# Experts' gate applied between their products, weight splits made at first use and tied behind the next input's chain, router's second rows in another buffer

## Chip, cores and metric

The kernel runs on one core of a Trainium2 chip. The metric is the time of one execution in microseconds (us) on the device. A core has a matrix engine (PE), three engines for elementwise work (DVE, ACT, POOL), and queues that issue transfers (SP's carries nearly all weights). Each engine works through its own instructions in the order in which the program lists them; semaphores hold an instruction until what it reads is there.

## The reference

Two networks one behind the other, on 256 rows of 1024 fp32 values:

```python
def first_block(x, mem, ...):
    h = rms_norm(x, attn_norm)
    ...                                   # attention, rwkv7, memory attention on h @ w_in
    x = x + mixed @ w_out
    xn = rms_norm(x, ffn_norm)
    return x + hierarchical_moe(xn, ...)

def hierarchical_moe(xt, ...):            # gate: [T, 16], two experts of one group per row
    for e in range(N_EXPERTS):
        hdn = silu(xt @ w_gate[e]) * (xt @ w_up[e])
        y = y + gate[:, e:e + 1] * (hdn @ w_down[e])
    return y

def swiglu(x, w1, w3, w2):
    return (silu(x @ w1) * (x @ w3)) @ w2
```

The second network adds six branches to the rows, each on its own rms_norm of them: a SwiGLU feed-forward of 2816 (ffn0), a mixer with 16 heads (hyb: dilated attention and top-k attention), ffn1, ffn2, a sliding-window attention (swa), ffn3. A last norm ends it.

## The kernel before

**Data.** The running rows are two tiles `h[0]`, `h[1]` of 128 x 1024 (`h_81`, `h_82` in the order's rows). All products keep fp32's accuracy by three matmuls (`mm3`, L105 to L107): each operand is a rounded high part and the rest, and the product is high x high, high x low, low x high. For the weights, `load` fetches a `raw` tile of 128 x 4096 through SP into a ring of three, and `split` cuts it into pieces of 1024 columns: ACT casts `wh` (L99), DVE subtracts to get `wl` (L100). A small ring of buffers holds the split pieces.

**Input of a branch.** `prep(...).fill(t)` makes a branch's input from `h[t]`: for each half `a` of its columns, PE transposes four blocks into a PSUM bank (L133), DVE multiplies by the norm's gain into `xf` (L139), ACT casts the high part `xh` (L140), DVE subtracts to get `xl` (L141). There are two such banks (`tr`), so the transposes of `h[1]` wait until `xf` of `h[0]` has been read out of them. Then ACT squares `h[t]` for the norm's divisor (L119). The divisor itself is applied later, where the product leaves PSUM.

**End of a branch.** `project_back` multiplies by the branch's last matrix, in an order of row blocks; the last `tail` of them (6 for all branches of the second network) are kept back, done for `h[0]` first and then for `h[1]`. Behind each, DVE adds the product to `h[t]` (L399, or L401 with a scale) and `after(t)` calls the next branch's `fill(t)`. It is a generator, and its first part (all but the tail) is started from `staggered`, which interleaves a mixer's head groups.

**Experts.** `moe` runs the 16 experts as eight pairs, each pair's 128 gathered rows as one tile. `first(p)` makes SiLU (ACT, L1348) times the up product (DVE, L1349) in `es`, transposes it into `eT`; `second(p, kept)` multiplies by the down matrix into two banks `po` (L1366), multiplies by the row's gate into `yf` (DVE, L1373), splits that in `yr` (cast on ACT L1374, subtraction on DVE L1375), and PE adds it back to the rows' places through the 0/1 matrix `PT` (L1380). After the eighth pair `add` adds the four sums to `h` (L1391), past a branch (L1401) that reads whether an expert overflowed its 64 slots.

**Order.** The program is written in Python order, but a scheduler with a model of the engines decides where an instruction stands in its engine's list. That list is fixed when the kernel is built.

## Time and profile before

| | |
|---|---|
| time, median of 3 runs | 1412.01 us (1409.84 to 1412.82) |
| time of the profiled execution | 1412.13 us |
| its span | 1410.4 us |
| PE busy | 1355.6 us (96%) |
| DVE busy | 743.6 us (53%) |
| ACT busy | 610.3 us (43%) |
| PE's idle time (span less busy) | 54.8 us |

The profile is of one execution. Its span is what the views divide; 1.7 us of the time lie around it. The branches lie in the span so: first network to 429 us (the experts from about 216), ffn0 to 630, hyb to 757, ffn1 to 945, ffn2 to 1131, swa to 1216, ffn3 to 1403.

### The profile page before, as it was taken

The page shows a single profiled execution, that of the slowest core. Times are in us where ns is not written, and L with a number is a line of the kernel's source. Part 1 is how long each engine was busy: PE and PEld are TensorE (multiplying, and loading weights), DVE is VectorE, ACT ScalarE, POOL GpSimd, SP SyncE. Part 2 cuts the span into 40 slices and gives each one's busy share as a digit, 9 for nine tenths or more (in the row PEclk, how much of TensorE's full clock was granted, in tenths as well). Part 3 has the DMA queues.
Part 4 walks back from the last instruction along what each step waited for, and adds up shares of the span by engine and source line. Part 5 has one row for each costly group of instructions (what it writes and reads, how often), then busy time and mean ns, then how long its engine had stood idle before and what let it go on. Part 6 is the DMA issues. An engine that isn't in the chain of part 4 may idle for free.

```text
span 1410.4 us, 18949 instructions
## 1 busy us (share of the span) xinstructions
PE 1355.6 (96%) x7650; PEld 1040.8 (74%) x7650; DVE 743.6 (53%) x1250; ACT 610.3 (43%) x961; POOL 73.9 (5%) x123
## 2 busy tenths in 40 slices
PE   7999889999998999999899999999999989999997
PEld 7787664343335888888787888888888878788886
DVE  6868641111126555456965555455545487555542
ACT  5545421011114444446565444445444376554442
POOL 1133100000000000000110000000000000000001
PEclk9999889999998999999999999999999999999999
DMA  8262579999964555446433555455554543355520
GB/s 318 91 236 92 211 285 412 412 415 425 425 277 180 185 180 199 157 157 254 150 120 127 202 181 207 150 186 198 206 183 152 209 164 135 140 210 183 199 90 30
DMA packets 35372, 293.82 MB, mean 208 GB/s; under 512 B 3729, under 2 KB 8113, under 8 KB 16081
## 3 DMA queue, kind: packets, MB, share of 16 engines
q1 hardware_dynamic: 29952, 286.58, 53.6%
q10 hardware_dynamic: 5328, 5.98, 1.3%
q8 instruction: 62, 1.02, 0.3%
q14 instruction: 30, 0.24, 0.0%
HBM read 291.45 MB, written 1.10 MB: 207 GB/s over the span
## 4 chain that ended last, share of the span: by engine, by line
PE 62%; DVE 5%; ACT 1%; issue 1%; POOLq 0%; ACTq 0%; POOL 0%
PE acc L105 19%; PE acc L107 19%; PE acc L106 19%; DVE wl L100 2%; PE tr L213 1%; PE acc L333 1%; ACT wh L99 1%; PE tr L325 1%; DVE xf L139 0%; DVE rep L534 0%; PE acc L295 0%; PE acc L296 0%; PE tr L133 0%; DVE m L533 0%; DVE sc L301 0%
## 5 line engine op out<-in xcount | busy, mean ns | idle before, releaser
L100 DVE TENSOR_TENSOR wl<-raw,wh 128x1024 fp32r<-128x1024 f32 (+1 forms) x349 | 426.2, 1224 | 362.7 <-ACT wh L99 358.4
L99 ACT CAST wh<-raw 128x1024 fp32r<-128x1024 f32 (+1 forms) x349 | 365.1, 1050 | 386.3 <-PE acc L107 330.8
L105 PE MATMUL acc<-wh,xh 128*128 128x512 f32 (+1 forms) x896 | 334.4, 374 | 2.8 <-ACT xh L140 2.2
L107 PE MATMUL acc<-wh,xl 128*128 128x512 f32 (+2 forms) x896 | 332.0, 371 | 1.0 <-DVE xl L141 1.0
L106 PE MATMUL acc<-wl,xh 128*128 128x512 f32 (+1 forms) x896 | 332.2, 371 | 0.0
L105 PEld LDWEIGHTS acc<-wh,xh 128*128 128x128 f32 x896 | 169.6, 189 | 31.3 <-ACT xh L140 2.6
L107 PEld LDWEIGHTS acc<-wh,xl 128*128 128x128 f32 x896 | 169.3, 189 | 30.4 <-DVE xl L141 2.3
L106 PEld LDWEIGHTS acc<-wl,xh 128*128 128x128 f32 x896 | 169.6, 189 | 28.2 <-DVE lent L766 0.6
L107 PE MATMUL acc<-wh,hl 128*128 128x512 f32 x352 | 137.6, 391 | 0.0
L106 PE MATMUL acc<-wl,hh 128*128 128x512 f32 x352 | 137.1, 389 | 0.0
L105 PE MATMUL acc<-wh,hh 128*128 128x512 f32 x352 | 137.0, 389 | 0.0
L107 PEld LDWEIGHTS acc<-wh,hl 128*128 128x128 f32 x352 | 66.1, 188 | 13.6
L105 PEld LDWEIGHTS acc<-wh,hh 128*128 128x128 f32 x352 | 66.1, 188 | 13.5
L106 PEld LDWEIGHTS acc<-wl,hh 128*128 128x128 f32 x352 | 66.1, 188 | 13.5
L105 PE MATMUL acc<-xh,wh 128*128 128x256 f32 x224 | 66.0, 296 | 1.5 <-ACT wh L99 0.8
L106 PE MATMUL acc<-xl,wh 128*128 128x256 f32 x224 | 64.6, 289 | 0.8 <-DVE xl L141 0.8
L107 PE MATMUL acc<-xh,wl 128*128 128x256 f32 x224 | 63.9, 288 | 0.0
L111 POOL TENSOR_SCALAR rstd<-ss 128x1 f32<-128x1 f32 x22 | 9.7, 439 | 954.6 <-ACT sq L119 702.2
L1340 PE MATMUL acc<-half,xe 128*64 128x512 f32 x248 | 59.6, 596 | 0.0
L1373 DVE TENSOR_SCALAR yf<-tr,gate 128x512 f32<-128x512 f32 x16 | 12.0, 752 | 81.0 <-PE tr L1366 80.8
L105 PEld LDWEIGHTS acc<-xh,wh 128*128 128x128 f32 x224 | 43.9, 196 | 4.8 <-issue 2.5
L106 PEld LDWEIGHTS acc<-xl,wh 128*128 128x128 f32 x224 | 44.0, 197 | 1.1 <-DVE xl L141 1.0
(450 smaller groups left out, 1656.0 us busy)
## 6 DMA issues: line engine op xcount, KB each, us to landing
raw<-in_ffn SPq DMA_DIRECT2D x63, 2048.0 KB, 7.9
half<-in_moe SPq DMA_DIRECT2D x45, 1024.0 KB, 13.7
raw<-in_moe SPq DMA_DIRECT2D x13, 2048.0 KB, 14.9
raw<-in_hyb SPq DMA_DIRECT2D x7, 2048.0 KB, 8.9
wl<-in_moe SPq DMA_DIRECT2D x23, 512.0 KB, 13.0
wh<-in_moe SPq DMA_DIRECT2D x23, 512.0 KB, 13.1
raw<-in_win SPq DMA_DIRECT2D x4, 2048.0 KB, 10.9
raw<-in_swa SPq DMA_DIRECT2D x4, 2048.0 KB, 8.8
```

The costliest lines, as they stand in the source:

```text
L99: nc.scalar.copy(hi[:, :n], x)
L100: nc.vector.tensor_tensor(lo[:, :n], x, hi[:, :n].bitcast(F32), OP.subtract)
L105: mm(out, a[0], b[0], start=start, stop=False)
L106: mm(out, a[0], b[1], start=False, stop=False)
L107: mm(out, a[1], b[0], start=False, stop=stop)
L111: self.nc.gpsimd.tensor_scalar(r, ss, eps, None, OP.add)
L213: nc.tensor.transpose(ps[:, i * 128:(i + 1) * 128], m[:, i * 128:(i + 1) * 128], self.ident)
L325: nc.tensor.transpose(pt[:, i * 128:(i + 1) * 128], s2[e][:, i * 128:(i + 1) * 128], self.ident)
L333: m = nc.tensor.matmul(po[64 * e:64 * e + 64, q], v[kb][:, c:c + 64], pT[e][:, z], start=kb == 0, stop=kb == 1)
L1340: last = mm(ps[c][e * 64:e * 64 + 64, :], xe[:, k, o + e * 64:o + e * 64 + 64], w[i][e][:, c * 512:c * 512 + 512], start=k == 0, stop=k == 7)
L1373: nc.vector.tensor_scalar(yf, po[a], gate[:, 0:1], None, OP.mult)
```

## The change

Five edits.

1. **Gate.** The product of gate and divisor is made once, in the small `gate` tile, and goes into `es` in place of the divisor alone. `po` is no longer multiplied: ACT casts `yr`'s high part straight from `po`, and DVE subtracts from `po`. The tile `yf` is gone.
2. **Splits at first use.** `project_back` loads all its raw tiles first and splits a piece where it is first multiplied.
3. **Ties.** `queue_behind` tells the scheduler that an instruction stands behind another; it adds no semaphore. After each branch the next ten splits are counted: the first two subtractions stand behind the last addition to `h[0]`, the third and fourth split behind the end of `fill(0)`, the fifth to tenth behind the end of `fill(1)`. The Square stands behind the fill's last cast.
4. **Staggered.** `project_back`'s first part is started after the last head group's first half, not ahead of it.
5. **Router.** The second rows' transposed tiles lie in a buffer of their own (`late`), and the router's logits and Squares stand behind two of the casts that follow.

```diff
     def split(self, x):
-        nc.scalar.copy(hi[:, :n], x)
-        nc.vector.tensor_tensor(lo[:, :n], x, hi[:, :n].bitcast(F32), OP.subtract)
+        both = (nc.scalar.copy(hi[:, :n], x),
+                nc.vector.tensor_tensor(lo[:, :n], x, hi[:, :n].bitcast(F32), OP.subtract))
+        self.nth += 1
+        if self.nth <= 2 and self.added:
+            self.queue_behind(both[1], self.added)
+        if 2 < self.nth <= 10:
+            for ins, other in zip(both, self.behind[self.nth > 4]):
+                self.queue_behind(ins, other)
         return hi, lo
+
+    def queue_behind(self, ins, other):
+        self.tc.add_manual_dep(ins.ins, other.ins.name,
+                               mybir.DependencyInfo(mybir.DependencyClass.NoSync, mybir.DependencyReason.DATA),
+                               reason="behind")
...
-            rs[t] = self.rms(h[t], D, 1.0 / 32)
+            rs[t] = self.rms(h[t], D, 1.0 / 32, ends[0])
+            return ends
...
-            if j + 1 == n:
-                next(then, None)
             rest = second(j, kept) or iter(())
             next(rest, None)
             kept = ahead
             if j + 2 < n:
                 prepare(j + 2)
+        next(then, None)
...
-        parts = {}
-        for b, src in enumerate(wsrc):
-            wd = self.load(src)
-            for i in sorted(range(src.shape[-1] // 1024), key=lambda i: order.index(4 * b + i)):
-                parts[4 * b + i] = self.split(wd[:, i * 1024:(i + 1) * 1024])
+        parts, raw = {}, [self.load(src) for src in wsrc]
 
         def one(t, k, a):
+            if k not in parts:
+                parts[k] = self.split(raw[k // 4][:, k % 4 * 1024:(k % 4 + 1) * 1024])
...
             gate = wk.tile([128, 2], F32, name=self.nm("gate"), tag="gate", bufs=2)
+            nc.vector.tensor_copy(gate[:, 1:2], pt[:, T + 2:T + 3])
             for e in range(2):
                 r = slice(64 * e, 64 * e + 64)
-                nc.vector.tensor_copy(gate[r, 0:1], pt[r, T + e:T + e + 1])
-            nc.vector.tensor_copy(gate[:, 1:2], pt[:, T + 2:T + 3])
+                nc.vector.tensor_tensor(gate[r, 0:1], pt[r, T + e:T + e + 1], gate[r, 1:2], OP.mult)
...
-            nc.vector.scalar_tensor_tensor(s, ps[1], gate[:, 1:2], s, OP.mult, OP.mult)
+            nc.vector.scalar_tensor_tensor(s, ps[1], gate[:, 0:1], s, OP.mult, OP.mult)
...
-                yf = self.wk.tile([128, 512], F32, name=self.nm("yf"), tag="xf")
                 yh, yl = yr[:, 2 * a], yr[:, 2 * a + 1]
-                nc.vector.tensor_scalar(yf, po[a], gate[:, 0:1], None, OP.mult)
-                nc.scalar.copy(yh, yf)
-                nc.vector.tensor_sub(yl, yf, yh.bitcast(F32))
+                nc.scalar.copy(yh, po[a])
+                nc.vector.tensor_sub(yl, po[a], yh.bitcast(F32))
```

The first place is DVE's list where the experts end and ffn0 begins, behind the branch on overflow. The first row is the end of that branch; `wl` is a weight split, `yr` the last pair's split, `h` the additions, `xf` and `xl` the next input. Before:

```order
L1401 UNCONDITIONAL_BRANCH
L100 TENSOR_TENSOR wl_3705<-raw_3387,wh_3704 128x1024
L1375 TENSOR_TENSOR yr_3365<-yf_3366,yr_3365 128x512
L1375 TENSOR_TENSOR yr_3365<-yf_3370,yr_3365 128x512
L1391 TENSOR_TENSOR h_81<-acc_2311,h_81 128x512
...
L100 TENSOR_TENSOR wl_3761<-raw_3756,wh_3760 128x1024
L139 TENSOR_TENSOR xf_3640<-tr_3635,cols 128x512
L100 TENSOR_TENSOR wl_3765<-raw_3756,wh_3764 128x1024
L139 TENSOR_TENSOR xf_3649<-tr_3644,cols 128x512
L100 TENSOR_TENSOR wl_3769<-raw_3756,wh_3768 128x1024
L100 TENSOR_TENSOR wl_3773<-raw_3756,wh_3772 128x1024
L141 TENSOR_TENSOR xl_3632<-xf_3640,xh_3631 128x4x128
```

And now, where the last pair's two `yr` stand ahead of the branch:

```order
L1425 UNCONDITIONAL_BRANCH
L1414 TENSOR_TENSOR h_81<-acc_2310,h_81 128x512
L1414 TENSOR_TENSOR h_82<-acc_2312,h_82 128x512
L1414 TENSOR_TENSOR h_81<-acc_2311,h_81 128x512
L1414 TENSOR_TENSOR h_82<-acc_2313,h_82 128x512
L155 TENSOR_TENSOR xf_3607<-tr_3602,cols 128x512
L155 TENSOR_TENSOR xf_3616<-tr_3611,cols 128x512
L156 TENSOR_TENSOR xl_3599<-xf_3607,xh_3598 128x4x128
L156 TENSOR_TENSOR xl_3599<-xf_3616,xh_3598 128x4x128
L155 TENSOR_TENSOR xf_3633<-tr_3628,cols 128x512
L155 TENSOR_TENSOR xf_3642<-tr_3637,cols 128x512
L101 TENSOR_TENSOR wl_3668<-raw_3354,wh_3667 128x1024
```

The splits of `raw_3756` (the second weight tile of ffn0; `raw_3723` now) stood between the additions and the first input; now none stands there, and the third piece of the first tile comes behind the second rows' `xf`.

The second place is DVE's list where swa ends and ffn3 begins (L399 and L413 are the additions). Before:

```order
L399 TENSOR_TENSOR h_82<-acc_9906,h_82 128x512
L399 TENSOR_TENSOR h_82<-acc_9907,h_82 128x512
L100 TENSOR_TENSOR wl_10200<-raw_10187,wh_10199 128x1024
L139 TENSOR_TENSOR xf_10030<-tr_10025,cols 128x512
L139 TENSOR_TENSOR xf_10039<-tr_10034,cols 128x512
L100 TENSOR_TENSOR wl_10204<-raw_10187,wh_10203 128x1024
L141 TENSOR_TENSOR xl_9254<-xf_10030,xh_9253 128x4x128
L141 TENSOR_TENSOR xl_9254<-xf_10039,xh_9253 128x4x128
```

And now:

```order
L413 TENSOR_TENSOR h_82<-acc_9885,h_82 128x512
L413 TENSOR_TENSOR h_82<-acc_9886,h_82 128x512
L155 TENSOR_TENSOR xf_9997<-tr_9992,cols 128x512
L155 TENSOR_TENSOR xf_10006<-tr_10001,cols 128x512
L156 TENSOR_TENSOR xl_9221<-xf_9997,xh_9220 128x4x128
L156 TENSOR_TENSOR xl_9221<-xf_10006,xh_9220 128x4x128
L155 TENSOR_TENSOR xf_10059<-tr_10054,cols 128x512
L155 TENSOR_TENSOR xf_10068<-tr_10063,cols 128x512
L101 TENSOR_TENSOR wl_10099<-raw_10086,wh_10098 128x1024
```

Two splits have left the chain from `h` to `xl`; the third piece of the new branch's first tile (`wl_10099`), which stood ahead of the additions to `h_81`, now stands behind the second rows' `xf`. At the end of hyb the same two splits leave the chain, and the transposes of `h_81` stand three matmuls ahead of the tail's end on PE.

The third place is DVE's list in the middle of hyb, where the top-k (L533, L534) and the first heads' `qa` and `ka` (L409) are interleaved. Before, the run of scores ends and then:

```order
L533 MAX m_1041_5564<-rep_5556 128x8
L409 SCALAR_TENSOR_TENSOR qa_5459<-acc_5434,bc_5125 128x256
L533 MAX m_1042_5567<-rep_5556 128x8
L534 MATCH_REPLACE rep_5563<-m_1041_5564,rep_5556 128x128
L534 MATCH_REPLACE rep_5563<-m_1042_5567,rep_5556 128x256
L100 TENSOR_TENSOR wl_5845<-raw_5834,wh_5844 128x1024
L533 MAX m_1044_5571<-rep_5563 128x8
L533 MAX m_1045_5574<-rep_5563 128x8
L409 SCALAR_TENSOR_TENSOR ka_5490<-acc_5465,bc_5125 128x256
```

And now:

```order
L426 SCALAR_TENSOR_TENSOR qa_5426<-acc_5401,bc_5092 128x256
L550 MAX m_1020_5524<-score_5394 128x8
L550 MAX m_1021_5527<-score_5394 128x8
L101 TENSOR_TENSOR wl_5812<-raw_5801,wh_5811 128x1024
L551 MATCH_REPLACE rep_5523<-m_1020_5524,score_5394 128x128
L551 MATCH_REPLACE rep_5523<-m_1021_5527,score_5394 128x256
L426 SCALAR_TENSOR_TENSOR ka_5457<-acc_5432,bc_5092 128x256
```

`qa` and `ka` are two top-k steps earlier in the list; the top-k's own steps are as many as before.

## Rows read from the trace of the kernel before

**Rows 1.** The page: busy time of the engines, and ACT's group of weight casts.

```profile
PE 1355.6 (96%) x7650; PEld 1040.8 (74%) x7650; DVE 743.6 (53%) x1250; ACT 610.3 (43%) x961; POOL 73.9 (5%) x123
...
L99 ACT CAST wh<-raw 128x1024 fp32r<-128x1024 f32 (+1 forms) x349 | 365.1, 1050 | 386.3 <-PE acc L107 330.8
```

**Rows 2.** PE's waits over the span: engine, line <- releaser: us, times, longest.

```profile
PE tr L133 <- DVE xf L139: 6.0, 3, 2.4
...
PE acc L295 <- DVE ka L409: 3.0, 2, 2.7
```

**Rows 3.** PE's timeline, experts to ffn0: start, length, instruction, [idle before <-releaser].

```profile
427.38 1.94 PE L1366 MATMUL tr<-raw,eT 128*64 128x512 f32 x8
...
434.31 2.07 PE L1380 MATMUL acc<-yr,PT 128*128 128x512 f32 x4 [1.82 <-DVE yr L1375]
...
442.72 0.80 PE L105 MATMUL acc<-wh,xh 128*128 128x512 f32 x1 [2.19 <-ACT xh L140]
...
444.44 0.78 PE L107 MATMUL acc<-wh,xl 128*128 128x512 f32 x1
```

**Rows 4.** DVE's timeline in the same stretch.

```profile
433.57 1.28 DVE L1375 TENSOR_TENSOR yr<-yf,yr 128x512 fp32r<-128x512 f32 x2
...
441.01 2.35 DVE L100 TENSOR_TENSOR wl<-raw,wh 128x1024 fp32r<-128x1024 f32 x2
```

**Rows 5.** ACT's timeline in the same stretch.

```profile
438.16 2.94 ACT L99 CAST wh<-raw 128x1024 fp32r<-128x1024 f32 x3 [5.50 <-SPq L1401]
441.01 1.05 ACT L119 ACTIVATE sq<-h 128x1024 bf16<-128x1024 f32 x1
...
442.06 0.60 ACT L140 CAST xh<-xf 128x512 fp32r<-128x512 f32 x1
```

**Rows 6.** Engines by groups, 216 to 440 us: busy, mean ns | idle before, releasers.

```profile
L1373 DVE TENSOR_SCALAR yf<-tr,gate 128x512 f32<-128x512 f32 x16 | 12.0, 752 | 81.0 <-PE tr L1366 80.8
L1375 DVE TENSOR_TENSOR yr<-yf,yr 128x512 fp32r<-128x512 f32 x16 | 11.0, 690 | 7.3 <-ACT yr L1374 7.1
...
L1239 DVE TENSOR_TENSOR xe<-tr,cols 128x512 f32<-128x512 f32 x6 | 4.1, 690 | 11.5 <-PE acc L1340 8.5 <-PE tr L1231 3.0
...
L1348 ACT ACTIVATE es<-acc,gate 128x512 f32<-128x512 f32 x8 | 5.5, 688 | 29.8 <-PE acc L1340 28.6 <-DVE gate L1324 1.1
```

**Rows 7.** Windows: busy of PE, PEld, DVE, ACT, POOL, granted clock, DMA share, GB/s.

```profile
440.00:447.00 7.00, 4.82 (x16) 3.60 (x15) 6.61 (x10) 5.44 (x10) 3.20 (x4) 0.52 0.94 377
...
757.00:761.00 4.00, 4.00 (x15) 3.00 (x16) 3.94 (x6) 1.69 (x4) 0.28 (x1) 0.57 0.42 82
...
1211.00:1218.00 7.00, 4.02 (x25) 2.92 (x24) 6.72 (x9) 4.62 (x7) 1.06 (x3) 1.00 0.70 288
```

**Rows 8.** PE's timeline, hyb to ffn1.

```profile
753.45 1.04 PE L133 MATMUL tr<-ident,h 128*128 128x128 f32 x8
...
759.23 0.76 PE L107 MATMUL acc<-wh,xl 128*128 128x512 f32 x1
```

**Rows 9.** DVE's timeline, swa to ffn3.

```profile
1213.62 1.22 DVE L100 TENSOR_TENSOR wl<-raw,wh 128x1024 fp32r<-128x1024 f32 x1
...
1217.09 1.29 DVE L141 TENSOR_TENSOR xl<-xf,xh 128x512 fp32r<-128x512 f32 x2
```

**Rows 10.** PE's timeline, swa to ffn3.

```profile
1217.83 0.50 PE L107 MATMUL acc<-wh,xl 128*128 128x512 f32 x1 [0.61 <-DVE xl L141]
1218.16 0.40 PE L105 MATMUL acc<-wh,xh 128*128 128x512 f32 x1
1218.40 0.39 PE L106 MATMUL acc<-wl,xh 128*128 128x512 f32 x1
```

**Rows 11.** DVE's timeline in hyb's middle.

```profile
670.50 0.62 DVE L533 MAX8 m<-score 128x8 f32<-128x128 f32 x2
...
673.18 1.24 DVE L100 TENSOR_TENSOR wl<-raw,wh 128x1024 fp32r<-128x1024 f32 x1
...
674.84 0.43 DVE L409 SCALAR_TENSOR_TENSOR ka<-acc,bc 128x256 f32<-128x256 f32 x1
```

More of the change, by code (lines that the diff above doesn't have):

```diff
@@ L38, in __init__ @@
         self.ahead, self.nsc = [], 3
+        self.nth, self.behind, self.added = 0, ((), ()), None
         self.n = 0
@@ L113, in rstd, with rms @@
         return r
-    def rms(self, x, n, scale):
+    def rms(self, x, n, scale, other=None):
         sq = self.wk.tile([128, D], BF16, name=self.nm("sq"), tag="sq", bufs=1)
         ss = self.wk.tile([128, 1], F32, name=self.nm("ss"), tag="ss", bufs=4)
-        self.nc.scalar.activation(sq[:, :n], x, AF.Square, scale=scale, accum_out=ss)
+        ins = self.nc.scalar.activation(sq[:, :n], x, AF.Square, scale=scale, accum_out=ss)
+        if other is not None:
+            self.queue_behind(ins, other)
+        self.squares = ins
         return self.rstd(ss, 1e-6)
@@ L139, in fill @@
                 nc.vector.tensor_tensor(xf, p3, g.unsqueeze(2).to_broadcast([128, 4, 128]), OP.mult)
-                nc.scalar.copy(dh, xf)
-                nc.vector.tensor_tensor(dl, xf, dh.bitcast(F32), OP.subtract)
-            rs[t] = self.rms(h[t], D, 1.0 / 32)
+                ends = [nc.scalar.copy(dh, xf), nc.vector.tensor_tensor(dl, xf, dh.bitcast(F32), OP.subtract)]
+            rs[t] = self.rms(h[t], D, 1.0 / 32, ends[0])
+            return ends
         return (xh, xl, rs), fill
@@ L390, in project_back @@
         yield
+        ends, added = [], None
         for t in range(2):
@@ L398, in project_back @@
                 if scale is None:
-                    nc.vector.tensor_add(h[t][:, s], y[t][a], h[t][:, s])
+                    last = nc.vector.tensor_add(h[t][:, s], y[t][a], h[t][:, s])
                 else:
-                    nc.vector.scalar_tensor_tensor(h[t][:, s], y[t][a], scale, h[t][:, s], OP.mult, OP.add)
-            after(t)
+                    last = nc.vector.scalar_tensor_tensor(h[t][:, s], y[t][a], scale, h[t][:, s], OP.mult, OP.add)
+            ends.append(after(t))
+            added = added or last
+        if ends[0]:
+            self.nth, self.behind, self.added = 0, ends, added
     def o_tiles(self):
@@ L1155, in fill @@
         def fill(t):
+            late = self.wk.tile([128, 8, T], F32, name="hT", tag="xl", bufs=1) if t else None
             hT = []
@@ L1158, in fill @@
                 ps = self.trp()
-                hT.append(self.wk.tile([128, 4, 128], F32, name=self.nm("hT"), tag="xf"))
+                hT.append(late[:, 4 * a:4 * a + 4, :128] if t else
+                          self.wk.tile([128, 4, 128], F32, name=self.nm("hT"), tag="xf"))
                 for i in range(4):
@@ L1168, in fill @@
             o = COLSM["rbias"][0]
-            nc.vector.scalar_tensor_tensor(L[:, t, :], ps[:, :20], rs[t], self.cm[:, o:o + 20], OP.mult, OP.add)
+            last = nc.vector.scalar_tensor_tensor(L[:, t, :], ps[:, :20], rs[t], self.cm[:, o:o + 20], OP.mult,
+                                                  OP.add)
+            self.routed = self.squares, last
         return (L, rs), fill
@@ L1210, in moe @@
         for t in range(2):
-            nc.scalar.copy(hx[t], h[t])
+            cast = nc.scalar.copy(hx[t], h[t])
             for s in (slice(0, 512), slice(512, 1024)):
-                tt(hy[t][:, s], h[t][:, s], hx[t][:, s].bitcast(F32), OP.subtract)
+                last = tt(hy[t][:, s], h[t][:, s], hx[t][:, s].bitcast(F32), OP.subtract)
+            self.queue_behind(self.routed[t], last if t else cast)
         def places(q):
@@ L1354, in first @@
             nc.scalar.copy(hT, pt)
-            return hT, PT, gate
+            return hT, PT
         def second(p, kept):
-            hT, PT, gate = kept
+            hT, PT = kept
             po = [self.trp(), self.trp()]
@@ L1387, in add @@
         x, after = follow()
+        ends = []
         for t in range(2):
@@ L1391, in add @@
                 self.nc.vector.tensor_add(h[t][:, s], y[t][a], h[t][:, s])
-            after(t)
+            ends.append(after(t))
+        self.nth, self.behind = 0, ends
         return x
```

## Prediction

> **What bounds the kernel now.** I read the page first: PE is busy for 1355.6 of 1410.4 us, DVE for half of the span and ACT for less [rows 1]. The products are the same before and after, matmul for matmul, so only PE's idle 54.8 us, and the stretches in which its clock is low, can be won. Next come PE's waits over the span: the reader is to see that long ones are few, and that they stand at the seams between branches, where the next input is made. Three waits for `xf` (L139) alone make 6.0 us, and one in hyb, for `ka`, makes 2.7 [rows 2]. Last, the timelines of PE, DVE and ACT at each seam, side by side: who has what in its list ahead of the chain that PE waits for.
>
> The longest seam is that from the experts to ffn0. PE's last product of the experts ends at 427.38 + 1.94 = 429.32; the third product of ffn0, the first to need `xl`, starts at 444.44, 15.1 us later, with 5 us of work in between [rows 3]. Two things stretch it. DVE has weight splits ahead of `yr` (433.57, 4 us after the bank was there) and ahead of `xl`: two of them hold it from 441.01 for 2.35 us [rows 4]. ACT stands for 5.50 us at a cast whose raw tile has only just been loaded, does three such casts and a Square, and starts `xh` at 442.06 [rows 5]; those casts are of ffn0's second weight tile, which PE doesn't need until 24 products on the first have been done.
>
> **The change part by part.** I walk each seam in the changed lists with the durations of before. A subtraction or product of 128 x 512 on DVE takes 0.69 us, a pair 1.29 [rows 6, 9], so each further one adds 0.60; a cast of `xh` 0.60, a weight cast 1.05, a Square 1.05 [rows 1, 5]; a weight subtraction 1.18, half of a pair's 2.35 [rows 4]. [...]
>
> *Experts to ffn0.* With P = 429.32: ACT casts the second `po` by P + 0.8 (0.69, as its SiLU from a bank [rows 6]), DVE subtracts by P + 1.5. PE's last two of the eight products follow the branch, to about P + 2.7 at 0.5 us each (four took 2.07 [rows 3]). The four additions end near P + 4.2, since the last two wait for those products. First `xf` P + 4.9, first `xh` and first product P + 5.5, second `xf` P + 5.5, first `xl` and third product P + 6.2. That is 8.9 us earlier. But the third piece of the first tile now stands behind the input: ACT does `xh` twice (P + 6.1), the Square (7.2), the cast (8.2), DVE the subtraction (9.4). The 14th product needs it, and at full clock would be due at P + 6.2 + 11 x 0.24 = P + 8.8. So it starts at P + 9.4; at the low clock, by 11 x 0.43, at P + 10.9. Before, with five steps at 0.43 and six at 0.24, it started at about P + 18.7. The seam gives 9.3 or 7.8 us; PE is idle for about half of it still, so I can't choose the clock, and take **8.6** (7.0 to 9.3). The load that ACT stood for lands at 438.16, P + 8.8; its pieces are due 24 products after the first, past P + 11, and stand behind the input now, so it costs nothing unless the whole seam became 3 us shorter than I think.
>
> *Middle of hyb.* DVE is busy without a gap here. Scores end at 670.50; `ka` is made at 674.84, and PE waits for it for 2.7 us [rows 2, 11]. In the new list `qa` (0.43, as `ka`), two MAX (0.62), one weight split (1.24) and two replacements (of the MAX's length, as I take them: 0.62) stand ahead of `ka`: 670.50 + 2.91 = 673.4, 1.4 us earlier. DVE's work is the same, and later waits of PE in hyb are for DVE again, so some comes back: **1.2** (0 to 2.5, the top with the whole wait gone).
>
> *hyb to ffn1.* The tail ended at 753.45 and the third product came at 759.23, 5.8 us later [rows 8]. Now eight transposes (1.04) stand inside the tail, so it ends at 754.5, while DVE adds `h_82`'s first half and makes both `xf` of `h_81` (done by about 754.8). The second addition follows (755.45), then `xl` (756.1): third product near 756.15, after the other transposes. That is 3.1 us earlier. For 4 us behind the old gap the clock was 0.57 [rows 7], which cost four products 0.2 us each; if it stays up, 0.8 more. Against that, the second rows' `xh` now stands behind a Square and two casts on ACT, up to 0.75 late. **3.0** (2.2 to 3.8).
>
> *swa to ffn3.* The additions end at 1213.62 [rows 9]. Two `xf` now follow at once, to 1214.9; a bank is free at 1214.3 and the last eight transposes go to 1215.4; `xl` is made by 1215.6; third product 1215.9, for 1217.83 [rows 10]: 1.9 earlier. The third piece (`wl_10099`) ends by 1218.8 (Square, cast, subtraction as above, from 1215.5) and is due at 1218.5: 0.3 back. **1.6** (1.0 to 2.3).
>
> *Gate.* Sixteen products of 752 ns leave DVE, 12.0 us [rows 6]. Nearly all of it is off PE's path: DVE idles for 81.0 us just ahead of them, waiting for the product itself, and the next pair's products cover the chain. The 0.75 counts once, in the seam above, where it is contained. Elsewhere 0.2 for a single wait on `yr`; bounds -1.0 and 1.5, since PE's list inside the experts is rearranged too. The small gate products are as many as the copies were. The subtraction now reads PSUM: `xe`, the same form from a bank, has 690 ns, just as `yr` from SBUF has [rows 6], so it costs nothing.
>
> [...]
>
> *No gain counted:* ffn0 to hyb and ffn1 to ffn2 (next to no waits before; the fills stand between products there), ffn2 to swa (0 to 1.0), the router (its lists are the same but for names) and the loads (SP's list is the same but for one swap).
>
> Sum: 8.6 + 1.2 + 3.0 + 1.6 + 0.2 = 14.6. The profiled execution took 1412.13, 0.1 above the median of the three runs: 1412.13 - 14.6 = 1397.5. The terms' bounds together give 9.2 to 20.4, so 1391 to 1403 is this case's own range.
>
> **The rivals.**
>
> *Late pieces (0.15).* The ties make the third to tenth pieces late by design. If ACT's list holds them up by 1 to 2 us at each seam, the gains of hyb's end and swa's end go, and the clock in ffn0 stays low: 7 to 8 us remain, 1404 to 1405. For it: in both walks the 14th product already waits. Against: DVE is idle for long stretches directly after each seam.
>
> *More than the seams (0.11).* PE's clock stays up in all of them, and the waits inside the experts shrink too: all upper bounds and a little more, 1387 to 1391. Against: a gap of 2.4 us was followed by a clock of 0.57 at hyb's end, though the same one at swa's end left it at 1.00 [rows 2, 7]. [...]
>
> *Slower: splits that PE has to wait for (0.05).* Made at first use, a piece that isn't ready when its product comes costs a cast and a subtraction, 2.2 us. Eight such pieces in the six branches' last products, 17.6 us, would eat the gain and 0.2% more: 1415 and up. Against: ACT's casts wait for PE to free their buffers for 330.8 us [rows 1], so pieces are made as early as the ring lets them, in either version.
>
> *No effect (0.07).* The waits only move: DVE's and ACT's work per seam is the same, and what is put behind an input is due soon after. Then all seams but a part of the first give back their gains: 1409.2 to 1414.8, that is within 0.2%, about what a measurement of this kernel can tell from no change.
>
> **The numbers.** Forecast 0.62, rivals 0.15, 0.11, 0.05 and 0.07. Faster holds the first three: 0.88; same 0.07; slower 0.05. The range reaches from the second rival's middle to just past the first's, 1388 to 1406.
>
> **What the changed profile would show.** PE's three waits for `xf` under 3 us together; ffn0's third product 6 to 7 us behind the experts' last, with no weight cast on ACT ahead of `xh`; a new short wait for `wl` at the 14th product of ffn0 and ffn3; PE's wait for `ka` under 1.2 us; DVE's busy time some 12 us less. I'm wrong if the third product of ffn0 still comes past P + 9, if PE waits for `wh` or `wl` inside a branch's last products, or if PE's waits in the experts grow by more than 2 us.

## The result and the profile after

| | before | after |
|---|---|---|
| time, median | 1412.41 us (4 runs, 1409.84 to 1413.19) | 1395.66 us (4 runs, 1394.56 to 1396.09) |
| profiled execution | 1412.13 us, span 1410.4 | 1394.56 us, span 1392.8 |
| PE busy / idle in the span | 1355.6 / 54.8 us | 1351.4 / 41.4 us |

The ratio of the medians is 0.9881, with an interval of 0.9869 to 0.9894: faster by 16.8 us, 2.2 more than forecast and inside the range. The profiled execution is the fastest of the four, 1.1 us under their median; that of before lies within 0.3 us of its median. Of the 17.6 us that the span lost, 13.4 are idle time of PE and 4.2 busy time, although the matmuls are the same 7650: a clock that falls less (mean granted clock 0.989 over the span, 0.981 before). DVE has 11.0 us less to do, of the 12 forecast. The page's line of busy times, for [rows 1]:

```profile
PE 1351.4 (97%) x7650; PEld 1035.3 (74%) x7650; DVE 732.6 (53%) x1234; ACT 603.0 (43%) x961; POOL 73.8 (5%) x123
```

PE's waits over the span, for [rows 2] (line <- releaser: us, times, longest):

```profile
PE acc L311 <- DVE ka L426: 2.5, 3, 1.0
PE acc L311 <- DVE qT L426: 2.1, 2, 2.0
...
PE tr L149 <- DVE xf L155: 1.1, 2, 0.5
...
PE acc L119 <- DVE wl L101: 0.5, 2, 0.3
```

The waits for `xf` have gone from 6.0 to 1.1 us. Those for `ka` are shorter each, but three instead of two. New are 0.5 us for `wl`, in two waits; the wait for `qT` in swa is 2.0 us long, 1.6 before.

The seam from the experts to ffn0, PE's timeline, for [rows 3]:

```profile
424.65 2.75 PE L1388 MATMUL tr<-raw,eT 128*64 128x512 f32 x12
427.33 2.81 PE L1400 MATMUL acc<-yr,PT 128*128 128x512 f32 x8
...
432.25 1.25 PE L149 MATMUL tr<-ident,h 128*128 128x128 f32 x8 [0.54 <-DVE xf L155]
433.26 0.48 PE L118 MATMUL acc<-wh,xh 128*128 128x512 f32 x1
...
433.81 0.40 PE L120 MATMUL acc<-wh,xl 128*128 128x512 f32 x1
...
436.75 0.50 PE L119 MATMUL acc<-wl,xh 128*128 128x512 f32 x1 [0.26 <-DVE wl L101]
```

DVE in the same stretch, for [rows 4]:

```profile
429.11 2.49 DVE L1414 TENSOR_TENSOR h<-acc,h 128x512 f32<-128x512 f32 x4 [0.35 <-PE acc L1400]
431.51 1.28 DVE L155 TENSOR_TENSOR xf<-tr,cols 128x512 f32<-128x512 f32 x2
```

And ACT, for [rows 5]:

```profile
432.28 1.16 ACT L156 CAST xh<-xf 128x512 fp32r<-128x512 f32 x2 [4.25 <-DVE xf L155]
433.35 1.05 ACT L132 ACTIVATE sq<-h 128x1024 bf16<-128x1024 f32 x1
```

The experts' last product ends at 424.65 + 2.75 = 427.40, which is P here. The additions end at P + 4.2 (forecast 4.2), the third product starts at P + 6.4 (6.2) and the 14th at P + 9.35 (9.4), after the short wait for `wl`. ACT now waits for `xf` ahead of `xh`, not for a transfer; the Square and the casts come behind.

The clock there (windows: length; busy time of PE, PEld, DVE, ACT, POOL; granted clock; DMA share; GB/s), for [rows 7], and in swa:

```profile
440.00:447.00 7.00, 7.00 (x32) 5.79 (x32) 7.00 (x7) 7.00 (x9) 0.00 (x0) 1.00 0.89 328
1134.00:1140.00 6.00, 6.00 (x31) 5.18 (x31) 4.12 (x26) 3.77 (x17) 0.00 (x0) 0.50 0.65 265
```

In ffn0 it is 1.00 where it was 0.52; in swa, where nothing was forecast, it is 0.50.

The ends of hyb, for [rows 8], and of swa, for [rows 10], in PE's timeline:

```profile
739.34 1.03 PE L149 MATMUL tr<-ident,h 128*128 128x128 f32 x8
...
742.68 0.50 PE L120 MATMUL acc<-wh,xl 128*128 128x512 f32 x1
...
1196.71 1.03 PE L149 MATMUL tr<-ident,h 128*128 128x128 f32 x8
1198.26 1.25 PE L149 MATMUL tr<-ident,h 128*128 128x128 f32 x8 [0.51 <-DVE xf L155]
...
1202.76 0.50 PE L119 MATMUL acc<-wl,xh 128*128 128x512 f32 x1 [0.24 <-DVE wl L101]
```

At hyb's end no wait is left; from the first transposes to the third product pass 742.68 - 739.34 = 3.3 us, with three products of the tail among them now, against 5.8.

**A ledger.** For each stage, how much earlier (-) or later (+) a matmul of PE starts than the matmul with the same running number did before, read from the two traces where PE's order is the same or nearly so (good to about 0.2 us; one profiled execution each). The gain of a seam or a stage is the step between two columns:

| start before, us | 230 | 410 | 480 | 620 | 665 | 725 | 800 | 1120 | 1180 | 1390 |
|---|---|---|---|---|---|---|---|---|---|---|
| stage | experts | their end | ffn0 | its end | hyb, ahead of `ka` | hyb, behind | ffn1 | ffn2 | swa, late | ffn3 |
| the change | -2.3 | -1.1 | -11.3 | -11.2 | -11.7 | -13.5 | -16.9 | -16.8 | -15.4 | -17.6 |
| e1: gate alone | -0.7 | 0.6 | 1.0 | 1.0 | 1.0 | 4.4 | 3.6 | 3.7 | 3.6 | 4.7 |
| e2: no ties | -2.3 | -1.1 | -0.5 | -0.5 | -0.5 | 2.7 | 2.0 | 2.0 | 1.8 | 2.8 |
| e3: no gate | 2.2 | 2.2 | -5.4 | -5.4 | -5.9 | -2.5 | -5.9 | -5.8 | -5.2 | -7.3 |
| e4: not staggered | -0.6 | 0.7 | -9.5 | -9.5 | -10.0 | -11.7 | -14.6 | -14.5 | -13.5 | -15.7 |
| e6: hyb pinned | 2.3 | 3.5 | -6.7 | -6.7 | -7.2 | -3.8 | -7.2 | -7.2 | -7.2 | -9.6 |
| e7: Square late | 1.9 | 3.1 | -7.2 | -7.2 | -7.7 | -6.1 | -9.9 | -9.5 | -8.7 | -11.0 |
| e9: swa pinned | -0.8 | 0.5 | -9.7 | -9.7 | -10.2 | -11.9 | -15.3 | -15.2 | -14.1 | -16.6 |
| e11: ties to the 4th | 1.8 | 3.0 | -5.6 | -5.6 | -3.5 | -5.2 | -6.5 | -5.9 | -1.6 | -1.1 |
| e12: no router edit | -1.8 | -0.5 | -10.6 | -10.6 | -11.1 | -12.8 | -16.2 | -16.1 | -14.7 | -16.9 |

The first column is chance, not the edits: up to 215 us PE, DVE and ACT have the same lists in the change, e3, e4, e6, e7, e9 and e11, and their profiles stand between 2.3 us ahead and 2.3 behind. So only steps are compared, not columns.

### The profile page after: what moved, and what is told of

Same layout as the page of the kernel before. It is cut to its first block, busy times and chain, and to the rows that moved or that the text cites. A ratio compares the mean times of both kernels' runs of the same rounds, so it can differ in the third digit from the quotient of the medians.

```text
span 1392.8 us, 18916 instructions
## 1 busy us (share of the span) xinstructions
PE 1351.4 (97%) x7650; PEld 1035.3 (74%) x7650; DVE 732.6 (53%) x1234; ACT 603.0 (43%) x961; POOL 73.8 (5%) x123
## 5 line engine op out<-in xcount | busy, mean ns | idle before, releaser
L100 ACT CAST wh<-raw 128x1024 fp32r<-128x1024 f32 (+1 forms) x349 | 361.3, 1047 | 347.2 <-PE acc L120 302.3
L118 PE MATMUL acc<-wh,xh 128*128 128x512 f32 (+2 forms) x896 | 332.5, 372 | 0.9 <-DVE CR L830 0.6
L119 PE MATMUL acc<-wl,xh 128*128 128x512 f32 (+2 forms) x896 | 331.4, 370 | 0.5 <-DVE wl L101 0.5
L120 PE MATMUL acc<-wh,xl 128*128 128x512 f32 (+1 forms) x896 | 331.1, 370 | 0.0
L118 PEld LDWEIGHTS acc<-wh,hh 128*128 128x128 f32 x352 | 66.1, 188 | 13.4
L1395 DVE TENSOR_TENSOR yr<-tr,yr 128x512 fp32r<-128x512 f32 x16 | 11.1, 692 | 92.4 <-ACT yr L1394 92.2
L156 ACT CAST xh<-xf 128x512 fp32r<-128x512 f32 x28 | 16.5, 619 | 70.2 <-DVE xf L155 70.1
## 6 DMA issues: line engine op xcount, KB each, us to landing
raw<-in_moe SPq DMA_DIRECT2D x13, 2048.0 KB, 15.2
wl<-in_moe SPq DMA_DIRECT2D x23, 512.0 KB, 13.5
wh<-in_moe SPq DMA_DIRECT2D x23, 512.0 KB, 13.5
raw<-in_win SPq DMA_DIRECT2D x4, 2048.0 KB, 11.3
```

Source lines behind the costliest of these rows:

```text
L100: both = (nc.scalar.copy(hi[:, :n], x), nc.vector.tensor_tensor(lo[:, :n], x, hi[:, :n].bitcast(F32), OP.subtract))
L118: mm(out, a[0], b[0], start=start, stop=False)
L119: mm(out, a[0], b[1], start=False, stop=False)
L120: mm(out, a[1], b[0], start=False, stop=stop)
L156: ends = [nc.scalar.copy(dh, xf), nc.vector.tensor_tensor(dl, xf, dh.bitcast(F32), OP.subtract)]
L1395: nc.vector.tensor_sub(yl, po[a], yh.bitcast(F32))
```

## The experiments

The theory was the prediction's: the seams were long because splits stood ahead of the next input, and the ties put them behind it. The rivals: that the gate edit shortened the seam, or that the gains in hyb and swa are the scheduler's new draw and owed to no edit. e1 is the kernel before with one edit; e2 to e12 are the changed kernel with one thing altered.

| | median, us | ratio to before, 95% |
|---|---|---|
| e1: gate alone | 1417.14 | 1.0034 (1.0021 to 1.0047) |
| e2: no ties | 1418.75 | 1.0050 (1.0035 to 1.0065) |
| e3: no gate | 1402.73 | 0.9930 (0.9908 to 0.9952) |
| e4: not staggered | 1396.43 | 0.9891 (0.9869 to 0.9913) |
| e5: swa pinned | 1396.49 | 0.9890 (0.9875 to 0.9905) |
| e6: hyb pinned | 1401.05 | 0.9917 (0.9901 to 0.9932) |
| e7: Square late | 1397.62 | 0.9895 (0.9880 to 0.9910) |
| e8: e5, e6 and e7 | 1399.65 | 0.9918 (0.9905 to 0.9932) |
| e9: swa pinned otherwise | 1396.66 | 0.9897 (0.9877 to 0.9917) |
| e10: e9 and Squares of ffn1 to ffn3 | 1395.89 | 0.9885 (0.9867 to 0.9902) |
| e11: ties to the 4th split | 1409.65 | 0.9982 (0.9971 to 0.9993) |
| e12: no router edit | 1395.90 | 0.9894 (0.9876 to 0.9911) |

**e1, the gate edit alone.**

```diff
-                nc.vector.tensor_scalar(yf, po[a], gate[:, 0:1], None, OP.mult)
-                nc.scalar.copy(yh, yf)
-                nc.vector.tensor_sub(yl, yf, yh.bitcast(F32))
+                nc.scalar.copy(yh, po[a])
+                nc.vector.tensor_sub(yl, po[a], yh.bitcast(F32))
```

> The kernel before with the gate's edit alone. Theory (order at the seams): the last pair's subtractions now stand ahead of the branch, but on ACT four casts of ffn0's second weight tile and a Square still stand ahead of xh, and on DVE four subtractions ahead of xl. That tile lands about 9 us after the experts' last product, as before, so the third product of ffn0 still comes 14 to 16 us behind it (15.1 before, 6.4 in the changed kernel), and the time is 1409 to 1413 us. Rival (the shorter chain from po to yr is what was won): the third product comes 6 to 9 us behind, the time is 1401 to 1404.

It was 4.8 us slower than before, where no change or a small gain was expected. ACT's timeline at the first seam:

```profile
438.30 1.04 ACT L99 CAST wh<-raw 128x1024 fp32r<-128x1024 f32 x1 [5.54 <-SPq L1399]
```

and PE's, there and in hyb:

```profile
426.27 2.75 PE L1366 MATMUL tr<-raw,eT 128*64 128x512 f32 x12
...
442.85 0.80 PE L105 MATMUL acc<-wh,xh 128*128 128x512 f32 x1 [4.54 <-ACT xh L140]
...
444.38 0.80 PE L107 MATMUL acc<-wh,xl 128*128 128x512 f32 x1 [0.31 <-DVE xl L141]
...
678.21 0.80 PE L295 MATMUL acc<-ka,qa 64*128 64x128 f32 x4 [3.06 <-DVE ka L409]
```

The third product comes 444.38 - 429.02 = 15.4 us behind the experts' last, as before (15.1): the input is ready sooner and PE waits 4.54 us for `xh` instead, because ACT still stands at the raw tile that lands at 438.3. The gate's 0.75 us is hidden by a transfer. The loss is elsewhere: 1.3 us within the experts and 3.4 in hyb (ledger). In hyb there is no edit, yet the scheduler has ordered DVE's list there otherwise than before, and the clock shows the loss. Windows of e1 in hyb's middle, then of the kernel before:

```profile
664.00:670.00 6.00, 5.58 (x37) 4.85 (x33) 6.00 (x14) 4.63 (x10) 0.00 (x0) 0.78 0.63 268
...
682.00:686.00 4.00, 4.00 (x26) 4.00 (x26) 2.92 (x19) 2.56 (x10) 0.00 (x0) 0.69 0.81 324
```

```profile
676.00:678.00 2.00, 2.00 (x11) 1.35 (x9) 2.00 (x9) 1.78 (x4) 0.00 (x0) 0.50 0.04 8
678.00:680.00 2.00, 2.00 (x16) 2.00 (x15) 2.00 (x16) 2.00 (x9) 0.00 (x0) 0.80 0.92 188
```

Matmul for matmul, e1's two waits for `ka` are 0.7 us longer together (3.7 against 3.0), and the low clock behind the first costs 1.3 more. The other 1.4 are lost by a low clock ahead of that wait, where the lists of PE, DVE and ACT are still those of before; so about 2 of the 3.4 us are the list's, and what lowered the clock ahead of it is not shown. Inside the experts, each of the nine kernels of the ledger that have the gate edit loses 1.2 or 1.3 us between the columns of 230 and 410, and the one without it (e3) loses none: that loss is the edit's. PE waits less there (4.7 us from 216 to 416 us with the change, 6.5 before and in e3), but it has another order of products, and they take longer; which ones was not tried.

**e2, no ties.** The ties' function returns at once; the other four edits stay.

```diff
     def queue_behind(self, ins, other):
+        return
         self.tc.add_manual_dep(ins.ins, other.ins.name,
```

> The changed kernel with all ties taken out (the other four edits stay). Theory: ffn0's third product at 14 to 16 us behind the experts, PE's waits for xf at the ends of hyb and swa back to about 2.4 us each, so 14 of the 16.8 us are lost: 1408 to 1412 us. Rival (gate and splits at first use carry the gain): 1396 to 1402.

It lost the whole gain and 6 us more (its profile is of its fastest run, 1415.22, and stands 2.3 us ahead at the start, so the ledger shows less, and where the rest of it goes is not shown). ACT's timeline:

```profile
436.92 1.04 ACT L100 CAST wh<-raw 128x1024 fp32r<-128x1024 f32 x1 [5.79 <-SPq L1426]
```

ACT stands at the raw tile again, and the third product is 443.00 - 427.38 = 15.6 us behind. At the ends of hyb and swa it wins 0.7 and loses 1.0 (ledger), where the change wins 3.4 and 2.2. In hyb its DVE list is e1's, with a `ka` wait of 3.03. So without the ties the other four edits together win nothing and cost 6 us. (The splits at first use have no run of their own: built without them, the changed kernel has the same lists on every engine, but for buffer numbers, so beside the ties this edit does nothing.)

**e3, no gate.** The gate edit is taken back, the ties stay.

```diff
-                nc.scalar.copy(yh, po[a])
-                nc.vector.tensor_sub(yl, po[a], yh.bitcast(F32))
+                nc.vector.tensor_scalar(yf, po[a], gate[:, 0:1], None, OP.mult)
+                nc.scalar.copy(yh, yf)
+                nc.vector.tensor_sub(yl, yf, yh.bitcast(F32))
```

> The changed kernel with the gate's edit undone, ties and all else kept. Theory: the seam keeps its order but the last pair's second yr stands behind the branch again and each pair's chain is one DVE product of 0.75 us longer: third product of ffn0 7.5 to 9 us behind the experts' last (6.4 with the gate), 1 to 2.5 us lost in all: 1396.5 to 1398.5. Rival (the gate carries the seam): 1402 to 1406.

PE's timeline:

```profile
429.61 1.94 PE L1388 MATMUL tr<-raw,eT 128*64 128x512 f32 x8
...
439.39 0.48 PE L120 MATMUL acc<-wh,xl 128*128 128x512 f32 x1
```

The third product is 439.39 - 431.55 = 7.8 us behind, as expected for the seam; the step from 410 to 480 is 7.6 us, against 10.2 with the gate. So the gate is worth 2.6 us at this seam once the ties are there, and nothing without them (e1's step is a loss of 0.4); with what it costs inside the experts, 1.4 are left. The time missed its expectation by 4 us and lies in the rival's range, but not for the rival's reason: the seam kept most of its gain, and hyb lost 3.4 us (ledger, 665 to 725) with a `ka` wait of 3.03, though the gate is not used there.

**e4, not staggered.** `project_back`'s first part is started where it was before.

```diff
+            if j + 1 == n:
+                next(then, None)
...
-        next(then, None)
```

> The changed kernel with project_back's first part started ahead of the last head group's first half, as before. It alters PE's list in hyb and swa and the seam at hyb's end (both additions to h_82 stand ahead of xf again, as at swa's end). Theory: that seam's third product comes about 3 us behind the tail where the changed kernel has 2.7, the rest is the same: 0.3 to 1.5 us lost, 1396 to 1397. Rival (hyb's own gain comes from the stagger): 1397.5 to 1400, with PE's wait for ka back above 2 us.

The step at hyb's end (725 to 800) is 2.9 instead of 3.4 us, with a short wait for `xf` (0.51) and one for `wl` (0.25), as at the other seams. In the median nothing can be told from it.

**e11, ties only to the fourth split.**

```diff
-        if 2 < self.nth <= 10:
+        if 2 < self.nth <= 4:
```

> The changed kernel with the ties of the fifth to tenth split taken out. At the experts' end four casts of ffn0's second weight tile then stand ahead of the second rows' xh on ACT, but behind the first rows'. Theory (a cast whose tile is still landing holds everything behind it): ffn0's third product as in the changed kernel, 6.4 us behind the experts' last; that tile lands about 9 us behind it and four casts take 4, so the second rows' input comes at 13 to 15 us, where it is due at about 12: a new wait of 1 to 3 us in ffn0. hyb's list changes too and may add 0 to 5 us, so the time is 1397 to 1404. Rival (the fifth to tenth tie does nothing): no new wait in ffn0, 1395 to 1396.5.

It is 14.0 us slower than the changed kernel, far more than expected; 0.18% of the time before is left of the gain. PE's waits:

```profile
PE acc L120 <- DVE xl L156: 3.8, 3, 2.1
PE tr L149 <- DVE xf L155: 3.4, 2, 2.8
PE acc L118 <- ACT xh L156: 3.1, 6, 1.2
PE tr L474 <- DVE xf L155: 2.5, 2, 1.3
```

These four make 12.8 us; the changed kernel has 1.3 us of such waits on the same four lines. DVE's timeline where swa begins shows what they are for:

```profile
1128.79 2.35 DVE L101 TENSOR_TENSOR wl<-raw,wh 128x1024 fp32r<-128x1024 f32 x2
...
1131.66 1.22 DVE L101 TENSOR_TENSOR wl<-raw,wh 128x1024 fp32r<-128x1024 f32 x1
...
1133.39 1.22 DVE L101 TENSOR_TENSOR wl<-raw,wh 128x1024 fp32r<-128x1024 f32 x1
1134.52 1.28 DVE L156 TENSOR_TENSOR xl<-xf,xh 128x512 fp32r<-128x512 f32 x2
```

Four splits, 4.8 us, lie between the additions and `xl`, with the two `xf` (left out) between them. ffn0's third product comes 6.4 us behind the experts' last, as with all the ties, and the second rows' `xh` is then waited for by 1.2 us, as the theory had it; that seam gives 8.6 instead of 10.2. But what was expected of ffn0 alone happened at the other branches too: 2.1 us are lost at hyb's start (620 to 665), where the change wins 0.5, ffn1's seam gives 1.3 instead of 3.4, 4.3 are lost from 1120 to 1180 instead of 1.4, and ffn3's seam loses 0.5 instead of giving 2.2. Most of what is left of the distance between the two profiles is their start.

**e12, no router edit.**

```diff
-                hT.append(late[:, 4 * a:4 * a + 4, :128] if t else
-                          self.wk.tile([128, 4, 128], F32, name=self.nm("hT"), tag="xf"))
+                hT.append(self.wk.tile([128, 4, 128], F32, name=self.nm("hT"), tag="xf"))
...
-            self.queue_behind(self.routed[t], last if t else cast)
```

> The changed kernel with the router's edit undone (second rows' tiles in the shared buffers, no ties at the router). One DVE row changes its place. Theory: nothing can be told, 1395 to 1396.5, and this is also a measure of what two kernels with the same lists differ by. Rival (the buffer freed the router's second rows): PE's wait for hT grows by over 1 us and the time by as much.

No difference; it serves as a control. The order is the changed kernel's on PE and ACT, and on DVE but for a few rows of the router at 189 to 194 us; two tiles lie in another buffer; and yet its profile stands 0.6 us apart at the experts' end: differences of this size between two profiled executions need no cause, and by the first column not much larger ones either.

**Attempts on what the profile after had left.** The swa wait first. DVE's timeline of the changed kernel shows what `qT` stood behind:

```profile
1130.75 2.35 DVE L101 TENSOR_TENSOR wl<-raw,wh 128x1024 fp32r<-128x1024 f32 x2
1133.02 0.42 DVE L475 COPY kT<-tr 128x256 f32<-128x256 f32 x1
1133.35 0.75 DVE L426 SCALAR_TENSOR_TENSOR qT<-acc,bc 128x256 f32<-128x256 f32 x2
```

and PE's the wait, behind which the clock is 0.50 (window above):

```profile
1133.82 0.80 PE L311 MATMUL acc<-kT,qT 64*128 64x128 f32 x4 [1.95 <-DVE qT L426]
```

e5 and e9 put both splits behind `qT` on DVE, and their casts on ACT behind the norm's products `cn` (e5) or behind `bc`'s copy (e9, shown).

```diff
+        def late(both):
+            self.queue_behind(both[0], self.bc_copy)
+            self.queue_behind(both[1], self.evacs[1])
+        self.evacs, self.pin = [], {11: late, 12: late}
```

> The changed kernel with one more tie in swa: the first two splits of its last product (nth 11 and 12) stand behind the second qT on DVE and behind the last cn on ACT. Theory (what swa loses, 1.7 us against before, is these two splits ahead of kT and qT, and then the low clock): PE's longest wait for qT falls from 2.0 to under 0.5 us, the products behind it run at the full clock, and the time is 1.7 to 3 us under the changed kernel's: 1392.7 to 1394. Rival (DVE has the same work there, the wait only moves to the first softmax): 1395 to 1396.

> As the earlier tie in swa, but the two casts stand behind bc's copy on ACT (in the earlier one they stood right ahead of it, and qT waited for bc). Theory (the two splits, on either engine, hold up the chain cn, kT, bc, qT): PE's first wait for qT under 0.7 us, no low clock behind it, 1.5 to 3 us under the changed kernel: 1392.7 to 1394.2. Rival (qT is bounded by something else, or what is saved is paid at the first softmax): 1395 to 1397.

In e5 the casts fell just ahead of `bc`, and PE's first wait for `qT` was 2.05 us. In e9 it was 0.92, with the clock at 1.00 from 1134 to 1140, and two other waits took its place:

```profile
1133.85 0.50 PE L313 MATMUL acc<-kT,qT 64*128 64x128 f32 x4 [0.92 <-DVE qT L429]
...
1139.52 1.27 PE L343 MATMUL tr<-ident,sc 128*128 128x128 f32 x6 [0.92 <-DVE sc L330]
...
1141.60 0.50 PE L313 MATMUL acc<-kT,qT 64*128 64x128 f32 x4 [0.82 <-DVE qT L429]
```

swa then loses 1.1 us (1120 to 1180) instead of 1.4: as the rival had it, where DVE's work stands in the list only moved the wait. The 1.4 is not the list's alone either. In e6, whose lists are the change's up to this wait, the same wait of 1.95 us is followed by a clock of 1.00, and swa loses nothing (ledger).

e6 did the same in hyb: two splits and the first MAX behind the second `ka`.

```diff
+        late = lambda both: self.queue_behind(both[1], self.evacs[3])
+        self.evacs, self.pin = [], {14: late, 15: late}
...
+                    if it == 0:
+                        self.queue_behind(ins, self.evacs[3])
```

> The changed kernel with ties in hyb: the top-k's first two MAX and the splits nth 14 and 15 stand behind the second ka on DVE. Theory (ka's place in DVE's list is what PE waits for): the longest wait for ka falls from 1.0 us to under 0.3, and 0.5 to 1.5 us are won: 1394 to 1395. Rival (DVE bounds hyb's middle, so the work pushed back is waited for next): waits for sc, pT or the next ka grow by as much, 1395 to 1397.

The first wait for `ka` went, and five splits gathered behind it, ahead of the next. DVE's timeline, then PE's:

```profile
665.57 5.75 DVE L102 TENSOR_TENSOR wl<-raw,wh 128x1024 fp32r<-128x1024 f32 x5
```

```profile
677.39 0.64 PE L313 MATMUL acc<-ka,qa 64*128 64x128 f32 x4 [5.03 <-DVE ka L429]
```

hyb gave 3.4 us away instead of winning 1.8, and the time lies above the range of the theory and of the rival.

e7 puts the Square behind the third and fourth split's casts in every feed-forward.

```diff
+        sq0 = self.sqs[0]
+        self.pin = {4: lambda both: self.queue_behind(sq0, both[0])}
```

> The changed kernel with h[0]'s Square tied behind the casts of the third and fourth piece in the four feed-forwards. Theory (the short wait at the 14th product is the Square ahead of that cast on ACT): PE's waits for wl L101 (0.5 us in two) go, 0.3 to 0.8 us won: 1394.9 to 1395.4, about what can be told from none. Rival (the wait is for DVE's list, two xf ahead of the subtraction): the waits stay and nothing is won.

The waits for `wl` at the 14th products of ffn0 and ffn3 shrank from 0.26 and 0.24 us to 0.10 and 0.06. hyb's list changed again (a `ka` wait of 4.15; 1.6 us lost there), so the median shows none of it. e8 joins e5, e6 and e7, e10 joins e9 with e7's edit for ffn1 to ffn3:

> The changed kernel with the three sets of ties together. If each does in company what its theory says alone: 2.5 to 5 us under the changed kernel, 1390.5 to 1393. If the lists shift elsewhere, as they did in hyb when only the gate's edit was undone, it is anywhere from 1391 to 1397.

> The tie in swa of the run above, and h[0]'s Square behind the casts of the third and fourth piece in ffn1, ffn2 and ffn3 alone, so that the lists ahead of hyb stay as in the changed kernel. Theory: 0.2 to 0.5 us under the run above, too little to be told from it, and no wait for wl at the 14th product of ffn3. Rival (the wait goes to the second rows' xh, as it seems to in the four feed-forwards): the same time within 0.2, with a wait for xh instead.

e8 has hyb's wait of 5.0 us and, with 1399.65, lies above its range; e10 is level with the changed kernel. No version beat it.

## Why the prediction was right

| step of the sum | forecast, us | ledger, us |
|---|---|---|
| experts to ffn0 | 8.6 (7.0 to 9.3) | 10.2 |
| middle of hyb | 1.2 (0 to 2.5) | 1.8 |
| hyb to ffn1 | 3.0 (2.2 to 3.8) | 3.4 |
| swa to ffn3 | 1.6 (1.0 to 2.3) | 2.2 |
| all else | 0.2 | 0.0 |

The seams, which make most of the sum, came by their mechanism. That the total came so close is in part luck: hyb's term had the wrong reason, and what I left out balances.

*Experts to ffn0.* The walk held to 0.2 us at the third and to 0.1 at the 14th product, and the mechanism is shown: without the ties the seam is as long as before (e2), with them and without the gate it gives 7.6 (e3). The size was off since I took the middle between full and low clock; it stayed at 1.00 (440 to 447 us), which the walk priced at 9.3. The walk's two steps from product to product, 0.43 and 0.24 us, are those of the kernel before; here PE's timeline and windows of it, where the 14th product starts at 448.10, P + 18.8:

```profile
445.02 0.63 PE L105 MATMUL acc<-wh,xh 128*128 128x512 f32 x1
445.44 0.63 PE L106 MATMUL acc<-wl,xh 128*128 128x512 f32 x1
445.87 0.63 PE L107 MATMUL acc<-wh,xl 128*128 128x512 f32 x1
...
447.86 0.40 PE L105 MATMUL acc<-wh,xh 128*128 128x512 f32 x1
448.10 0.39 PE L106 MATMUL acc<-wl,xh 128*128 128x512 f32 x1
448.33 0.40 PE L107 MATMUL acc<-wh,xl 128*128 128x512 f32 x1
```

```profile
444.00:446.00 2.00, 2.00 (x8) 1.71 (x7) 1.74 (x3) 0.64 (x2) 1.52 (x3) 0.50 1.00 377
...
448.00:450.00 2.00, 2.00 (x11) 1.63 (x10) 0.00 (x0) 0.00 (x0) 0.00 (x0) 1.00 0.92 393
```

They are 0.43 us apart at a clock of 0.50 and 0.23 to 0.24 at 1.00. Eleven steps at the low clock behind the tied input, which made the 7.8 and so the middle of 8.6, were my estimate and are shown by no run: from 440 to 447 us the clock was 1.00 in e3 and e11, too, and 0.50 and 0.52 in e1 and e2, which have no ties. The rest is that P itself moved forward by 0.8 more than the products ahead of it (1.9 us, where the ledger has 1.1 at 410): the products from there to P stand in another order, with no wait in either kernel. That is the gate edit's, since e1 has it and e3 has not. I counted the gate's 0.75 as contained in the seam; e1 shows that alone it is worth nothing there, and e3 that behind the ties it is 2.6.

*Middle of hyb.* The number came out, the reason did not. I took it from a shorter wait for `ka`. The single waits are under 1.2 us, as said, PE's timeline in hyb:

```profile
661.97 0.50 PE L311 MATMUL acc<-ka,qa 64*128 64x128 f32 x4 [1.01 <-DVE ka L426]
...
670.44 0.61 PE L341 MATMUL tr<-ident,sc 128*128 128x128 f32 x3 [0.94 <-DVE sc L328]
```

but they are three now, 2.5 us in all against 3.0, and one for `sc` has come. Matmul for matmul, the first wait is 1.7 us shorter (I had walked to 1.4), the products behind it are 1.5 us quicker, since they ran at the low clock before (0.50 from 676 to 678), and the later waits give 1.4 back. So the waits alone are worth 0.3, where I counted 1.2, and the clock, which I didn't count, makes up the rest: that is luck. After the change the clock is 1.00 throughout hyb's middle (656 to 704 us). Nor is the gain owed to one edit: e1, e2, e3 and e7 each got another DVE list in hyb, with waits of 3.0 to 4.2 us, and lost 1.6 to 3.4 us there (1.4 of it in e1 and e2 ahead of where their list differs from before), while e4, e9, e11 and e12 kept the list and the gain. That list is the scheduler's, and any edit ahead of it may change it.

*hyb to ffn1, swa to ffn3.* Right by mechanism. At hyb's end the third product came 3.1 us earlier, as walked, and the clock stayed at 1.00 (739 to 745 us), which I had priced at 0.8 and left out: 3.4. (That it stayed up need not be the shorter gap's doing: in e1 it stayed up there behind the old gap, see the last section.) At swa's end the third piece cost a wait of 0.24, as forecast (0.3), and the input was a little sooner. The waits for `xf` at both fell to 0.51 or nothing.

*All else.* It balances by accident: 2.3 us from the experts' start, 1.2 of it given back inside them, 0.5 won at hyb's start ("no gain counted": PE's waits of 0.9 and 0.3 us there became one of 0.5), and 1.4 lost in swa, which I had not foreseen: the walk stopped at the seams, and I didn't look where swa's own evacuations stand in the new list. The start is this execution's chance (first column), and by the median, 1.1 us above it, all else is a loss of about 1. What is given back inside the experts is the gate's price, by e1, e3 and the other kernels of the ledger; so the term of 0.2 for the gate elsewhere was wrong in sign and measured -1.2, below its lower bound of -1.0.

*The gate's subtraction from PSUM.* DVE's group in the changed kernel, 216 to 430 us:

```profile
L1395 DVE TENSOR_TENSOR yr<-tr,yr 128x512 fp32r<-128x512 f32 x16 | 11.1, 692 | 92.4 <-ACT yr L1394 92.2
```

692 ns against 690 from SBUF [rows 6]: free for this form, as taken from the rows.

*The rivals.* "Late pieces" showed as two waits of 0.26 and 0.24 us, not 1 to 2. "More than the seams" came halfway: the clock stayed up at three seams (1.00 in 440 to 447, 739 to 745 and 1197 to 1203) and the waits inside the experts shrank, but its products there took longer, and the clock fell in swa (0.50 in 1134 to 1140). "Slower" did not happen: no wait for `wh` or `wl` inside a branch's last products. "No effect" is nearly what e11 shows: with four ties instead of ten the waits did move, and nearly all of them came back.

## What to carry to other kernels

Look at what stands ahead of a chain in each in-order list before making the chain itself shorter: here a cast that waited for its transfer (5.54 us in e1) hid the saving behind it (0 against 2.6 us at the seam for the same gate edit), and the work to be moved was all that stood there, not the first few pieces (with ten splits tied 1.2% were won, with four of them 0.2%). Where a scheduler makes the lists, read the lists of stages that the edit doesn't touch, too: here hyb's was worth 1.8 us one way and about 2 the other. A change is then judged only together with its draw, and an experiment that takes one edit out needs its lists compared before its time is read as that edit's worth. And profiled executions with the same lists stood up to 4.6 us apart here (2.3 ahead to 2.3 behind); compare steps between two places, not the places themselves.

## What the runs showed of the hardware

The granted clock fell to 0.50 behind some waits and not behind others. In hyb's middle the difference is clear: behind six waits for `ka` of 2.7 us and more (before, e1 to e3, e6, e7) it was 0.50 to 0.61 in the first us, behind the waits of 1.0 in the change and in e4 it was 1.00; in e9 to e12 the four products behind such a wait took 0.50 us, as in the change, against 0.80 before. Elsewhere the same wait went both ways. A gap of 2.38 us before was followed by 0.57 at hyb's end and by 1.00 at swa's [rows 7]; in e1, with the same DVE rows, it was the other way round. PE's timeline of e1 and its windows:

```profile
761.22 1.25 PE L133 MATMUL tr<-ident,h 128*128 128x128 f32 x8 [2.37 <-DVE xf L139]
...
1219.12 1.25 PE L133 MATMUL tr<-ident,h 128*128 128x128 f32 x8 [2.37 <-DVE xf L139]
```

```profile
761.00:765.00 4.00, 3.17 (x16) 2.34 (x17) 4.00 (x7) 1.48 (x3) 0.57 (x1) 1.00 0.37 70
...
1222.00:1226.00 4.00, 4.00 (x15) 3.21 (x14) 2.49 (x4) 1.22 (x2) 0.00 (x0) 0.78 0.86 336
```

That is all of the 1.1 us that e1 loses at swa's end. In swa, ahead of the same products on 64 rows, the clock fell after 1.95 us in the change (0.50; the first four products took 0.80 us there, and 0.81 after 1.95 in e12) and after 2.05 in e5 (0.62 and 0.52 in the next four us), and stayed at 1.00 after 1.95 in e6, 1.60 before and 0.92 in e9; after 2.17 in e11 the four products took 0.50 us, as in e6. PE's timeline of e6 and the window behind it:

```profile
1143.44 0.50 PE L313 MATMUL acc<-kT,qT 64*128 64x128 f32 x4 [1.95 <-DVE qT L429]
```

```profile
1144.00:1150.00 6.00, 5.61 (x45) 4.64 (x41) 5.15 (x32) 5.27 (x22) 0.00 (x0) 1.00 0.87 328
```

In hyb's middle a wait of 0.42 us for `qb` was followed by 1.00 before and by 0.78 in e1 (664 to 670 us). So for the waits of about 2 us here nothing that the lists show decided the clock behind them, and a loss of that kind in one profile, such as the 1.4 us in swa (0.6 to 1.4 in the change, e3, e4, e7 and e12, 0.0 in e6, all with a wait of 1.9 to 2.0), can't be put down to a list by itself. What decides is left open. The price in hyb's middle, matmul for matmul: from the first product behind the wait to the next transposes of `sc` pass 6.72 us in the change, 8.23 before, behind 2.71 us, and 9.50 in e1, behind 3.06, so 1.5 and 2.8 more.
